# Queries and keys copied out of their banks unscaled, values split at once, and one ordinary step moved in the order of the last part

## The chip, the core and the metric

The kernel runs on one core of one Trainium2 chip. A core has a matrix engine (TensorE, in the profile PE, with PEld for its weight loads), a vector engine (VectorE, DVE), a scalar engine (ScalarE, ACT), GpSimd (POOL) and a queue that issues the transfers (SyncE, SP). The metric is the device time of one execution in microseconds (us); smaller is better.

## What is computed

One encoder block for 256 tokens of width 2048, in float32. The input is normalised and projected once into the heads of three attention mixers and three gates; the mixers are added under their gates, projected, and followed by a SwiGLU feed-forward part of inner width 5632. The reference, cut down:

```python
h = rms_norm(x, g_mix)
qa, ka, va, qb, kb, vb, qc, gt = split(h @ w_in)
qa, ka = rms_norm(split_heads(qa), g_qa), rms_norm(split_heads(ka), g_ka)
oa = mixture of three dilated windows of (qa, ka, va) with rel_bias        # 6 heads
qb, kb = rope(rms_norm(split_heads(qb), g_qb)), rope(rms_norm(split_heads(kb), g_kb))
ob = softmax(qb kb^T / sqrt(128)) vb                                       # 6 query, 2 key heads
kc, vc = split(rms_norm(mem, g_mem) @ w_mem_kv);  kc = rms_norm(kc, g_kc)
oc = softmax(rms_norm(qc, g_qc) kc^T / sqrt(128)) vc                       # 4 heads
merged = sum over branches of sigmoid(gate) * (o @ w_br)
x = x + merged @ w_o
hf = rms_norm(x, g_ffn) @ w_ffn_in
x = x + (silu(hf[:DFF]) * hf[DFF:]) @ w_ffn_out
```

A row's normalisation is a factor per token, so the kernel multiplies with the unscaled x first and applies the factor to the result.

## The kernel before

**Products.** A float32 operand is split into a high and a low part (`split`, lines 128 to 132: ScalarE makes the high part, VectorE the low one), and every product is made of three matmuls: high by high, high by low, low by high. A weight tile of 128 x 1024 comes by DMA into one of six `raw` buffers and is split into `whi` and `wlo`. A plain `product` accumulates two halves of 128 tokens into two banks of 128 x 512. All instructions come from helpers that record the operation, so PE and DMA rows of the trace carry line 75.

**Banks.** There are eight banks of 128 x 512 values, four under the tag "mm" (results of products) and four under "at" (transposes, scores, attention's results). A bank can take its next result when the last reader of the old one is done.

**Stages.** First the memory's keys and values (one `pair`), then eight products for queries, keys and values, each of four heads (`SLOTS`), two gate products with a small branch product each, then, from about 330 us on, the merging of gates and branches, the output projection and the feed-forward part. From there on PE's order is that of the program. Before, while attention runs beside the projections, a scheduler sets each engine's order by its own estimate; `tc.high_priority()` raises what stands under it.

**Heads.** When a product ends, `take_slots` takes its four heads. Queries and keys: ScalarE squares the bank into `sq` (line 576), VectorE sums the squares (577), and once the token factors are known makes `f`; ScalarE reads the bank again, scaled by `f`, into `y` (591); GpSimd applies the gain (612) or VectorE turns the head (604 to 609); PE transposes it (`hT`), and the split gives `headT`. Values are split straight from the bank into `V`, scaled by the token factor (the loop behind `y = rot if turned else y`). The steps between two `yield` run at a tick of the running product; `EVAC_LAG` is three ticks.

**Attention.** `attend` makes scores (`sc`) from two `headT`, the softmax (`pr`), transposes it (`pT`, by `turn`), splits that, and multiplies with `V` into `o`, whose split is `oT`.

**Pairs with seven products.** Behind the early part, `pair` works through a list of steps such as STEPS_LAST. `d` and `D` are ordinary steps (12 matmuls for one weight tile; d into the banks Y and V, D into Z and Q). `f`, `g`, `h`, `p`, `q` make a 2 x 2 block product out of seven products in place of eight: f3, g3 and h3 make the first five for block 3, p0 the sixth and q0 the seventh. f, p and q all use bank X: what p has left there is copied by ScalarE (line 433, `SB`) before q may begin. A step's loads and splits are issued up to four steps ahead of its matmuls. The last part, `feeding` with `last`, has two pairs, both by STEPS_LAST; their results go to x, and out of the core by DMAs in the same queue as the weights.

Of the kernel before, what the change touches and what calls it, by code (L numbers as in the profile page):

```python
# [12 lines left out]
F32R = mybir.dt.float32r  # L13
I32 = mybir.dt.int32
AF = mybir.ActivationFunctionType
ALU = mybir.AluOpType
AX = mybir.AxisListType

P = 128
S = 256  # L20
T = S // P
D = 2048
KT = D // P
HD = 128
# [5 lines left out]
HEAD_LAG, SM_LAG, EVAC_LAG, PV_LAG = 5, 6, 3, 2  # L30
# [24 lines left out]
STEPS_FFN = "d0 D0 d1 D1 d4 D4 f2 d5 g2 D5 h2 f3 d6 g3 h3 p0 D6 q0 d7 D7".split()  # L55
STEPS_O = "d0 D0 d1 D1 f2 d4 g2 D4 h2 d5 f3 D5 g3 d6 h3 p0 D6 q0 d7 D7".split()
STEPS_OUT = "d0 D0 d1 D1 d2 D2 f6 d3 g6 D3 h6 f7 d4 g7 h7 p0 D4 q0 d5 D5".split()
STEPS_LAST = "d0 f2 D0 g2 d1 h2 D1 f3 d4 g3 D4 h3 p0 q0 d5 D5".split()
STEPS_OUT2 = "d0 f5 D0 g5 d1 h5 f6 D1 g6 d2 h6 f7 D2 g7 d3 h7 p0 p2 D3 q0 q2 d4 D4".split()


# [38 lines left out]
def encoder_block(ctx: ExitStack, tc: tile.TileContext, a: dict, out: bass.AP):  # L100
    nc = InOrder(tc)
# [16 lines left out]
    def s4(shape, name, dt=F32):  # L118
        return mid.tile(shape, dt, name=name, tag="s4")

    def bank(name, tag="at"):
        return psum.tile([P, NC], F32, name=name, tag=tag)


    def split(hi, lo, src, scale=None):

        if scale is None:
            nc.scalar.activation(hi, src, AF.Copy)  # L128
            nc.vector.tensor_sub(lo, src, hi.bitcast(F32))  # L129
        else:  # L130
            nc.scalar.activation(hi, src, AF.Copy, scale=scale)
            nc.vector.scalar_tensor_tensor(lo, src, scale, hi.bitcast(F32), op0=ALU.mult, op1=ALU.subtract)  # L132

    def rsqrt(v, shape):

        y = small.tile(shape, F32, name="rs_y")
        h = small.tile(shape, I32, name="rs_h")
        nc.vector.tensor_scalar(h, v.bitcast(I32), 1, None, op0=ALU.logical_shift_right)
        nc.vector.tensor_scalar(y.bitcast(I32), h, -1.0, float(0x5F3759DF), op0=ALU.mult, op1=ALU.add)
        for _ in range(3):  # L140
            t = small.tile(shape, F32, name="rs_t")
            y2 = small.tile(shape, F32, name="rs_y")
            nc.vector.scalar_tensor_tensor(t, y, -0.5, y, op0=ALU.mult, op1=ALU.mult)
            nc.vector.tensor_mul(t, t, v)
            nc.vector.scalar_tensor_tensor(y2, t, 1.5, y, op0=ALU.add, op1=ALU.mult)
            y = y2
        return y
# [104 lines left out]
    known = set()  # L252
# [311 lines left out]
    headT, V = {}, {}  # L564
    s2 = heads.enter_context(tc.tile_pool(name="s2", bufs=16))

    def take_slots(ps, slots, r, name="x"):

        n = sum(s[0][0] != "v" for s in slots)
        if n:  # L570
            y = s4([P, T, 4, HD], "y")
            sq = s4([P, T, 4, HD], "sq")
            ss = small.tile([P, T, 4], F32, name="hss")
            for t in range(T):
                src = ps[t][:, :n * HD].rearrange("p (n d) -> p n d", d=HD)
                nc.scalar.activation(sq[:, t, :n], src, AF.Square)
            nc.vector.tensor_reduce(ss[:, :, :n], sq[:, :, :n], axis=AX.X, op=ALU.add)
            yield EVAC_LAG
        while name not in known:
            yield None  # L580
        if n:
            v = small.tile([P, T, 4], F32, name="hv")
            f = small.tile([P, T, 4], F32, name="hf")
            each = lambda w: r[:, w].unsqueeze(2).broadcast_to([P, T, n])
            nc.vector.tensor_mul(ss[:, :, :n], ss[:, :, :n], each(1))
            nc.vector.tensor_scalar(v[:, :, :n], ss[:, :, :n], 1.0 / HD, EPS, op0=ALU.mult, op1=ALU.add)
            nc.vector.tensor_mul(f[:, :, :n], rsqrt(v[:, :, :n], [P, T, n]), each(0))
            yield EVAC_LAG
            for t in range(T):
                for j in range(n):  # L590
                    nc.scalar.activation(y[:, t, j], ps[t][:, j * HD:(j + 1) * HD], AF.Copy, scale=f[:, t, j:j + 1])
            turned = slots[0][0][1] == "b"
            rot = s4([P, T, 4, HD], "rot") if turned else None
            j = 0
            while j < n:
                m = 1
                while j + m < n and slots[j + m][0] == slots[j][0]:
                    m += 1
                if turned:
                    tab = turns[:, ("qb", "kb").index(slots[j][0])]  # L600
                    for t in range(T):
                        cs, sn = (tab[:, w, t].unsqueeze(1).broadcast_to([P, m, HD]) for w in range(2))
                        yt, other = y[:, t, j:j + m], sq[:, t, j:j + m]
                        nc.vector.tensor_mul(rot[:, t, j:j + m], yt, cs)
                        pairs = lambda v: v.rearrange("p n (d c) -> p n d c", c=2)
                        for c in range(2):
                            nc.vector.tensor_mul(pairs(other)[:, :, :, c], pairs(yt)[:, :, :, 1 - c],
                                                 pairs(sn)[:, :, :, c])
                        nc.vector.tensor_add(rot[:, t, j:j + m], rot[:, t, j:j + m], other)
                else:  # L610
                    g = gh[:, HEAD_GAINS.index(slots[j][0])]
                    nc.gpsimd.tensor_mul(y[:, :, j:j + m], y[:, :, j:j + m],
                                         g.unsqueeze(1).unsqueeze(1).broadcast_to([P, T, m, HD]))
                j += m
            y = rot if turned else y
        for i in range(n, len(slots)):
            v = s2.tile([P, 2, T, HD], F32R, name="V", tag="s2")
            V[slots[i]] = v
            for t in range(T):
                split(v[:, 0, t], v[:, 1, t], ps[t][:, i * HD:(i + 1) * HD], r[:, 0, t:t + 1])  # L620
        if n:
            yield HEAD_LAG
            for j in range(n):
                tp = bank("hT")
                for t in range(T):
                    nc.tensor.transpose(tp[:, t * P:(t + 1) * P], y[:, t, j], ident)
                hT = s2.tile([P, 2, S], F32R, name="headT", tag="s2")
                with tc.high_priority():
                    split(hT[:, 0], hT[:, 1], tp[:, :S])
                headT[slots[j]] = hT  # L630
                if j % 2 and j < n - 1:
                    yield 1
        yield 2
        run_jobs()
# [68 lines left out]
    def run_jobs():  # L703
        while jobs and all(s in headT for s in jobs[0][0] + jobs[0][1]):
            q, k, v, kt = jobs.pop(0)
            start(attend(q, k, v, bias[kt] if kt < 2 else None, kt))
# [5 lines left out]
    def beginning():  # L712
        start(hold(6, row_sums(a["mem"], r_m, 3, "mem")))
        start(hold(10, constants()))
        start(hold(5, fetch(xT, 2)))
        yield pair(block_pair(a["w_mem"], 0), memT, whole_k(KT // 2),
                   lambda c, r: start(take_slots(r, MEM_SLOTS[4 * c:4 * c + 4], r_m, "mem")), operand=memT)
# [4 lines left out]
    for c in range(8):  # L722
        sums = {} if c else {0: row_sums(a["x"], r_x, 4, "x")}
        start(take_slots(product(a["w_qkv"][c], xT, KT, beside=sums), SLOTS[4 * c:4 * c + 4], r_x))
        if c == 0:
            start(biases())
# [41 lines left out]
    def by_pair(these, room):  # L768
        return lambda u, f: (room[these.index(u)][:, 0, (f + 1) % 4], room[these.index(u)][:, 1, (f + 1) % 4])
# [80 lines left out]
    def feeding():  # L850
        for c0, c1 in ((0, 4), (4, 8), (8, KF // 4)):
# [27 lines left out]
            if last:  # L879
                pairs = STEPS_LAST, STEPS_LAST  # L880
                out_forms = by_pair((2, 3), late)
# [114 lines left out]
```

## Time and profile before

| what | value |
|---|---|
| median of 3 runs | 1385.53 us (1384.79 to 1386.54) |
| the profiled execution | 1386.69 us, its span 1384.9 us |
| granted TensorE clock, mean | 0.997 |
| PE busy | 1373.3 us, 99% of the span |
| VectorE, ScalarE busy | 1176.1 us, 829.0 us |
| weights and inputs read | 273.05 MB, 199 GB/s over the span |

How to read it: a timeline row is start, length, engine, line, operation, output<-input, sizes, and in brackets how long the engine sat idle before it and what ended that. Matmuls overlap: a row's length is longer than the distance to the next start. A row of waits is "who waits <- for whom: us in total, times, longest". A row of windows gives the stretch and each engine's busy time in it, then the granted clock, the DMA share and GB/s. A row of groups gives busy us and mean ns behind the first bar, idle us and what ended it behind the second. SPq is the queue of transfers.

### The profile page before, as it was taken

How to read it: one execution, taken by the hardware profiler on the slowest of the kernel's cores; microseconds unless marked ns; L12 is line 12 of the kernel's file. 1: busy time of each engine (PE TensorE's matmuls, PEld its weight loads, DVE VectorE, ACT ScalarE, POOL GpSimd, SP SyncE). 2: the span in 40 equal slices, each digit the busy share in tenths (PEclk: the TensorE clock that was granted, in tenths of full speed). 3: DMA queues.
4: the chain of work that ended last, by engine and by line, in shares of the span. 5: the costliest groups of instructions: out<-in, count | busy, mean ns of one | idle time of the engine just before them, and what ended most of it. 6: DMA issues, size and time to landing. Idle time of an engine off the chain costs nothing.

```text
span 1384.9 us, 17667 instructions
## 1 busy us (share of the span) xinstructions
PE 1373.3 (99%) x6249; PEld 1137.6 (82%) x6249; DVE 1176.1 (85%) x1665; ACT 829.0 (60%) x1131; POOL 14.2 (1%) x14
## 2 busy tenths in 40 slices
PE   9999999999999999999999999999999999999998
PEld 7878878888888888888888888888888888888886
DVE  6869777859988978888988898989998989998997
ACT  7766555655665564656766565655665665566653
POOL 0010001000000000000000000000000000000000
PEclk9999999999999999999999999999999999999999
DMA  9876435556565665755656665665655656565654
GB/s 370 310 244 210 138 126 173 159 162 194 193 231 187 185 229 174 278 170 180 198 183 201 211 192 187 197 213 198 223 186 184 226 179 205 189 202 194 203 169 150
DMA packets 79721, 277.10 MB, mean 200 GB/s; under 512 B 9040, under 2 KB 11600, under 8 KB 79376
## 3 DMA queue, kind: packets, MB, share of 16 engines
q1 hardware_dynamic: 79488, 275.94, 60.6%
q8 instruction: 49, 0.80, 0.2%
q14 instruction: 40, 0.33, 0.1%
q10 hardware_dynamic: 144, 0.02, 0.0%
HBM read 273.05 MB, written 2.88 MB: 199 GB/s over the span
## 4 chain that ended last, share of the span: by engine, by line
PE 97%; DVE 1%; ACT 1%; DMA 0%; issue 0%; SPq 0%; DVEq 0%
PE mmZ L75 17%; PE mmV L75 17%; PE mmY L75 17%; PE mm L75 16%; PE mmQ L75 14%; PE mmX L75 10%; PE mmW L75 3%; PE tp L75 1%; PE sc L75 1%; PE o L75 1%; PE hT L75 0%; DMA raw<-in_w_mem 0%; DVE wlo L129 0%; PE pT L75 0%; ACT whi L128 0%
## 5 line engine op out<-in xcount | busy, mean ns | idle before, releaser
L383 ACT ACTIVATE whi<-raw 128x1024 fp32r<-128x1024 f32 (+1 forms) x480 | 473.6, 998 | 339.1 <-PE mmQ L75 96.7
L393 DVE TENSOR_TENSOR wlo<-raw,whi 128x1024 fp32r<-128x1024 f32 (+1 forms) x480 | 543.0, 1146 | 75.8 <-ACT whi L383 70.5
L75 PE MATMUL mm<-whi,xT 128*128 128x512 f32 x640 | 204.3, 395 | 0.5 <-DVE V L132 0.5
L129 DVE TENSOR_TENSOR wlo<-raw,whi 128x1024 fp32r<-128x1024 f32 x82 | 103.5, 1266 | 52.5 <-ACT whi L128 51.4
L75 PEld LDWEIGHTS mm<-whi,xT 128*128 128x128 f32 x640 | 120.3, 189 | 25.5 <-DVE V L132 1.1
L128 ACT ACTIVATE whi<-raw 128x1024 fp32r<-128x1024 f32 x82 | 86.8, 1065 | 70.1 <-PE mm L75 51.4
L75 PE MATMUL mm<-wlo,xT 128*128 128x512 f32 x320 | 126.4, 395 | 0.0
L393 DVE TENSOR_TENSOR wlo<-t,whi 128x1024 fp32r<-128x1024 f32 x82 | 81.0, 1003 | 40.0 <-ACT whi L383 39.5
L75 PE MATMUL mmY<-whi,x1T 128*128 128x512 f32 x288 | 103.0, 390 | 0.0
L383 ACT ACTIVATE whi<-t 128x1024 fp32r<-128x1024 f32 x82 | 70.5, 877 | 51.2 <-PE mmV L75 31.3
L75 PE MATMUL mmV<-whi,x1T 128*128 128x512 f32 x288 | 100.2, 392 | 0.0
L75 PE MATMUL mmX<-whi,forms 128*128 128x512 f32 x260 | 88.1, 390 | 1.4 <-ACT SB L433 1.4
L75 PE MATMUL mmZ<-whi,x1T 128*128 128x512 f32 x224 | 78.3, 390 | 0.0
L75 PE MATMUL mmQ<-whi,x1T 128*128 128x512 f32 x224 | 78.1, 389 | 0.0
L75 PEld LDWEIGHTS mm<-wlo,xT 128*128 128x128 f32 x320 | 60.7, 190 | 12.5 <-issue 0.7
L75 PEld LDWEIGHTS mmY<-whi,x1T 128*128 128x128 f32 x288 | 54.1, 188 | 11.3
L75 PEld LDWEIGHTS mmV<-whi,x1T 128*128 128x128 f32 x288 | 54.1, 188 | 11.0
L75 PEld LDWEIGHTS mmX<-whi,forms 128*128 128x128 f32 x260 | 48.8, 188 | 12.3 <-ACT SB L433 2.2
L75 PE MATMUL mmV<-wlo,x1T 128*128 128x512 f32 x144 | 56.1, 389 | 0.0
L75 PE MATMUL mmY<-wlo,x1T 128*128 128x512 f32 x144 | 56.0, 389 | 0.0
L75 PE MATMUL mmW<-whi,forms 128*128 128x512 f32 x130 | 51.6, 397 | 0.2 <-DVE x1T L132 0.2
L75 PE MATMUL mmY<-whi,hT 128*128 128x512 f32 x148 | 51.8, 389 | 0.0
(266 smaller groups left out, 2762.4 us busy)
## 6 DMA issues: line engine op xcount, KB each, us to landing
raw<-in_w_ffn SPq DMA_DIRECT2D x176, 512.0 KB, 4.4
raw<-in_w_gate SPq DMA_DIRECT2D x96, 512.0 KB, 4.3
raw<-in_w_ffn_out SPq DMA_DIRECT2D x88, 512.0 KB, 4.4
raw<-in_w_qkv SPq DMA_DIRECT2D x64, 512.0 KB, 4.3
raw<-in_w_o SPq DMA_DIRECT2D x32, 512.0 KB, 4.2
raw<-in_w_br SPq DMA_DIRECT2D x24, 512.0 KB, 4.5
raw<-in_w_mem SPq DMA_DIRECT2D x15, 512.0 KB, 8.0
rawT<-in_memT SPq DMA_DIRECT2D x8, 256.0 KB, 7.6
```

Of the source, the lines that this page charges most:

```text
L75: ins = op(*args, **kw)
L128: nc.scalar.activation(hi, src, AF.Copy)
L129: nc.vector.tensor_sub(lo, src, hi.bitcast(F32))
L383: nc.follow(nc.scalar.activation(hi[:, o], v, AF.Copy))
L393: nc.follow(nc.vector.tensor_sub(*due.pop(0)))
```

## The change

Two things. In `take_slots`, queries and keys are now copied out of their bank as they are, each directly behind its squares (line 578), and scaled from that copy in place (line 601). Squares, copies and their sum are under high priority. The values' split is moved ahead of the scaling, to the place where the token factors are known, and is under high priority too. The lag of three ticks ahead of the factors falls away where these are known already, and one stands now between the values and the rest. In STEPS_LAST, f3 stands one step earlier, and the ordinary step D4 is moved from between g3 and h3 to between p0 and q0.

```diff
-STEPS_LAST = "d0 f2 D0 g2 d1 h2 D1 f3 d4 g3 D4 h3 p0 q0 d5 D5".split()
+STEPS_LAST = "d0 f2 D0 g2 d1 h2 f3 D1 g3 d4 h3 p0 D4 q0 d5 D5".split()
...
-            for t in range(T):
-                src = ps[t][:, :n * HD].rearrange("p (n d) -> p n d", d=HD)
-                nc.scalar.activation(sq[:, t, :n], src, AF.Square)
-            nc.vector.tensor_reduce(ss[:, :, :n], sq[:, :, :n], axis=AX.X, op=ALU.add)
+            with tc.high_priority():
+                for t in range(T):
+                    src = ps[t][:, :n * HD].rearrange("p (n d) -> p n d", d=HD)
+                    nc.scalar.activation(sq[:, t, :n], src, AF.Square)
+                    nc.scalar.activation(y[:, t, :n], src, AF.Copy)
+                nc.vector.tensor_reduce(ss[:, :, :n], sq[:, :, :n], axis=AX.X, op=ALU.add)
+        if name not in known:
             yield EVAC_LAG
         while name not in known:
             yield None
+        with tc.high_priority():
+            for i in range(n, len(slots)):
+                v = s2.tile([P, 2, T, HD], F32R, name="V", tag="s2")
+                V[slots[i]] = v
+                for t in range(T):
+                    split(v[:, 0, t], v[:, 1, t], ps[t][:, i * HD:(i + 1) * HD], r[:, 0, t:t + 1])
         if n:
+            yield EVAC_LAG
...
-                    nc.scalar.activation(y[:, t, j], ps[t][:, j * HD:(j + 1) * HD], AF.Copy, scale=f[:, t, j:j + 1])
+                    nc.scalar.activation(y[:, t, j], y[:, t, j], AF.Copy, scale=f[:, t, j:j + 1])
...
-        for i in range(n, len(slots)):
-            v = s2.tile([P, 2, T, HD], F32R, name="V", tag="s2")
-            V[slots[i]] = v
-            for t in range(T):
-                split(v[:, 0, t], v[:, 1, t], ps[t][:, i * HD:(i + 1) * HD], r[:, 0, t:t + 1])
```

Since a scheduler orders the early part, the order of the engines there changes in many places; from the merging on, up to the last part's two pairs, it stays the same on PE, ScalarE and VectorE. Three places follow.

PE, the head pair of mixer B that shares its product with the first value head; before:

```order
L75 MATMUL mm<-whi,xT 128x512
L75 MATMUL o<-pT,V 128x256
L75 MATMUL pT<-ident,pr 128x128 x4
L75 MATMUL o<-pT,V 128x256 x5
L75 MATMUL pT<-ident,pr 128x128 x4
L75 MATMUL o<-pT,V 128x256
L75 MATMUL mm<-whi,xT 128x512
```

The same heads in the changed program:

```order
L75 MATMUL pT<-ident,pr 128x128 x2
L75 MATMUL o<-pT,V 128x256 x5
L75 MATMUL pT<-ident,pr 128x128 x6
L75 MATMUL mm<-whi,xT 128x512
L75 MATMUL mm<-wlo,xT 128x512
L75 MATMUL mm<-whi,xT 128x512 x2
...
L75 MATMUL mm<-wlo,xT 128x512
L75 MATMUL o<-pT,V 128x256
```

Between the transposes of the softmax (pT) and the product with the values (o) there were no matmuls of the projection; now there are 20.

PE, the last query heads of mixer B; hT is the transpose of the last query, sc its scores; before:

```order
L75 MATMUL pT<-ident,pr 128x128 x4
L75 MATMUL o<-pT,V 128x256 x7
L75 MATMUL hT<-ident,rot 128x128 x2
L75 MATMUL o<-pT,V 128x256 x5
L75 MATMUL sc<-headT 128x256 x2
L75 MATMUL mm<-whi,xT 128x512
```

The same heads in the changed program:

```order
L75 MATMUL pT<-ident,pr 128x128 x8
...
L75 MATMUL mm<-wlo,xT 128x512
L75 MATMUL o<-pT,V 128x256
L75 MATMUL hT<-ident,rot 128x128 x2
L75 MATMUL mm<-whi,xT 128x512 x2
L75 MATMUL mm<-wlo,xT 128x512
L75 MATMUL o<-pT,V 128x256 x11
...
L75 MATMUL mm<-whi,xT 128x512
L75 MATMUL sc<-headT 128x256 x2
```

There are 22 matmuls of the projection between pT and the first o now, and between hT and sc ten of them beside the eleven of o.

PE, the end of the last part's pairs (mmX is the bank of p0 and q0); before:

```order
L75 MATMUL mmX<-wlo,forms 128x512
L75 MATMUL mmX<-whi,forms 128x512 x2
L75 MATMUL mmX<-wlo,forms 128x512
L75 MATMUL mmX<-whi,forms 128x512
L75 MATMUL mmY<-whi,hT 128x512
```

And in the changed program:

```order
L75 MATMUL mmX<-wlo,forms 128x512
L75 MATMUL mmX<-whi,forms 128x512
L75 MATMUL mmZ<-whi,hT 128x512
L75 MATMUL mmZ<-wlo,hT 128x512
...
L75 MATMUL mmQ<-whi,hT 128x512
L75 MATMUL mmX<-whi,forms 128x512
L75 MATMUL mmX<-wlo,forms 128x512
```

The 12 matmuls of D4 (Z and Q) stand between the last one of p0 and the first one of q0, which followed each other before.

In the transfer queue two of the three stores of a bias row (`flat`) had one weight load between them and the loads that fetch the row back; now these follow it directly.

## The prediction

> **What bounds the kernel now.** I read the page first, then the waits of TensorE (PE) and of the load queue, then the timeline wherever two PE starts stand further apart than the work between them.
>
> ```profile
> PE 1373.3 (99%) x6249; PEld 1137.6 (82%) x6249; DVE 1176.1 (85%) x1665; ACT 829.0 (60%) x1131; POOL 14.2 (1%) x14
> 50.57 17.67 PE mm L75 x78
> PE o L75 <- DVE pT L129: 1.7, 2, 0.9
> PE mmX L75 <- ACT SB L433: 1.4, 2, 0.7
> PE sc L75 <- ACT headT L128: 1.0, 1, 1.0
> PE mm L75 <- DVE V L132: 0.5, 2, 0.3
> ```
>
> PE bounds the span, and the change takes no matmul away, so only time that PE loses can be won. The second row (a piece of the chain of waits: 78 matmuls in 17.67 us) gives the undisturbed pace: 0.227 us for 512 columns. For 256 columns I take half, 0.113 us, an estimate. The waits, last number the longest, are short and few. But a wait's figure is idle time against modelled ends, so I measure what each costs by starts: time from start to start less the work between.
>
> **The places where PE loses time, and what the change does to each.**
>
> First place, the second projection of x begins:
>
> ```profile
> 71.94 0.39 PE L75 MATMUL mm<-whi,xT 128*128 128x512 f32 x1
> 72.58 0.50 PE L75 MATMUL mm<-whi,xT 128*128 128x512 f32 x1 [0.26 <-DVE V L132]
> 72.92 0.39 PE L75 MATMUL mm<-wlo,xT 128*128 128x512 f32 x1
> ```
>
> Two starts take 0.98 us where 2 x 0.227 would do: 0.53 us lost. PE waits for a bank that the split of the memory's last value head still reads; the other bank in question was held by the keys until they were scaled. Now the keys leave their bank directly after the squares, nine weight tiles earlier in ScalarE's order, so the product can begin in that bank and asks for the one of the values some matmuls later. I count 0.53 as gone (bounds 0 and 0.53).
>
> Second place, attention:
>
> ```profile
> 153.71 0.60 PE L75 MATMUL pT<-ident,pr 128*128 128x128 f32 x4
> 154.99 0.39 PE L75 MATMUL o<-pT,V 128*128 128x256 f32 x1 [0.68 <-ACT pT L128]
> 155.61 0.50 PE L75 MATMUL mm<-whi,xT 128*128 128x512 f32 x1 [0.23 <-DVE V L132]
> 155.95 0.39 PE L75 MATMUL mm<-wlo,xT 128*128 128x512 f32 x1
> ```
>
> Third place, attention again, with its consequence:
>
> ```profile
> 182.40 0.40 PE L75 MATMUL mm<-whi,xT 128*128 128x512 f32 x1
> 182.64 0.60 PE L75 MATMUL pT<-ident,pr 128*128 128x128 f32 x4
> 182.99 0.36 PE L75 MATMUL o<-pT,V 128*128 128x256 f32 x1
> 184.12 0.98 PE L75 MATMUL o<-pT,V 128*128 128x256 f32 x6 [0.76 <-DVE pT L129]
> 184.94 0.38 PE L75 MATMUL hT<-ident,rot 128*128 128x128 f32 x2
> 185.52 0.68 DVE L129 TENSOR_TENSOR pT<-pT 128x512 fp32r<-128x512 f32 x1
> 186.25 1.18 PE L75 MATMUL o<-pT,V 128*128 128x256 f32 x5 [0.94 <-DVE pT L129]
> 188.44 0.79 PE L75 MATMUL sc<-headT 128*128 128x256 f32 x2 [1.01 <-ACT headT L128]
> 189.03 0.66 PE L75 MATMUL mm<-whi,xT 128*128 128x512 f32 x1
> 193.33 0.44 PE L75 MATMUL mm<-wlo,xT 128*128 128x512 f32 x1
> 170.00:195.00 25.00, 22.30 (x108) 18.45 (x106) 20.07 (x67) 12.71 (x32) 0.00 (x0) 0.86 0.39 125
> ```
>
> Four transposes take 0.35 us (182.64 to 182.99). Second place: 153.71 to 155.95 is 2.24 us for 0.35 + 0.113 + 0.227, so 1.55 us lost. Third place: 182.40 to 193.33 is 10.93 us for one matmul (0.227), four transposes (0.35), twelve of `o` (1.36), two of `hT` (0.175), two of `sc` (0.227) and the ten from 189.03 to 193.33 (2.27): 4.60 us, so 6.33 us lost. Of these 2.03 us are those ten at 0.43 us each; the window's row shows why, a granted clock of 0.86 over 25 us.
>
> Why PE waits here: `o` stands directly behind the transposes whose result it multiplies, and that result must first pass ScalarE and VectorE. From the start of the transposes (182.64) to the end of VectorE's part (185.52 + 0.68) it took 3.56 us, 3.2 us from their end. The order of the changed program (front part) puts 20 matmuls of 512 columns between transposes and `o` at the second place, 4.5 us, and 22 at the third, 5.0 us, both above 3.2. Between the query's last `hT` and `sc` there now stand 10 of 512 columns and 11 of 256: 3.5 us where there were five of 256, 0.6 us. I count both as gone, 1.55 and 6.33 us (bounds 0 and these sums).
>
> Fourth and fifth place, the last part's pairs, where the seventh product (q0) needs the bank from which the sixth (p0) is being copied:
>
> ```profile
> 1340.32 0.39 PE L75 MATMUL mmX<-whi,forms 128*128 128x512 f32 x1
> 1341.39 0.50 PE L75 MATMUL mmX<-whi,forms 128*128 128x512 f32 x1 [0.69 <-ACT SB L433]
> 1341.73 0.40 PE L75 MATMUL mmX<-wlo,forms 128*128 128x512 f32 x1
> 1372.58 0.39 PE L75 MATMUL mmX<-whi,forms 128*128 128x512 f32 x1
> 1373.65 0.50 PE L75 MATMUL mmX<-whi,forms 128*128 128x512 f32 x1 [0.69 <-ACT SB L433]
> 1373.99 0.40 PE L75 MATMUL mmX<-wlo,forms 128*128 128x512 f32 x1
> 1355.93 1.18 SPq L75 DMA_DIRECT2D raw<-in_w_ffn_out  x2
> ```
>
> Each: 1.41 us for two starts, less 0.453: 0.96 us, together 1.91 us. The ordinary step D4 puts 12 matmuls, 2.7 us, over a copy that PE waits for until 1.07 us after the last start; I count all of it. D4's weights are not late: the very last loads of the kernel are issued by 1357.1, 15 us before p0 ends. f3 comes one step earlier, but between it, g3, h3 and p0 there stand as many ordinary steps as before.
>
> **What is added, and what hides it.** Sixteen copies on ScalarE, of the shapes of the squares, and the 56 scalings read SBUF where they read a bank:
>
> ```profile
> L576 ACT ACTIVATE sq<-mm 128x512 f32<-128x512 f32 (+2 forms) x14 | 7.0, 548 | 2.0 <-PE mm L75 1.8
> L591 ACT ACTIVATE y<-mm,hf 128x128 f32<-128x128 f32 x48 | 13.1, 385 | 0.0
> sum 325.00, PE 319.17 PEld 266.12 DVE 237.65 ACT 200.41 POOL 14.19; mean PE 26.60 PEld 22.18 DVE 19.80 ACT 16.70 POOL 1.18
> ACT whi L128 <- PE mm L75: 51.4, 35, 5.9
> ```
>
> 14 squares take 7.0 us, so 16 copies about 8 us. ScalarE is busy 200 of the first 325 us, and its weight splits alone wait 51 us for PE, so 8 us find room: zero on the path. If that cover were gone at a block, one block's two copies, about 1.1 us, would show. A scaling from SBUF has no row; I take the 385 ns from a bank, and even twice that, 21 us more over 325 us, would stay under PE. The value splits keep their number and only come sooner.
>
> **Sum.** 0.53 + 1.55 + 6.33 + 1.91 = 10.3 us. The new order also has some fifteen new places where attention is taken up, and the cheapest wait above cost 0.5 us; I let one such come back: 9.8 us. The profiled execution took 1386.69 us (span 1384.9), 1.16 above the median 1385.53; from that median I forecast 1375.7 us.
>
> **Rivals.** First, the half clock has another cause. Matmuls at half pace came after waits of which none was longer than about 1.0 us, and the two waits of 0.7 us at the end brought none. If it falls anyway, 2.03 us stay: 1377.7 us. [...] The trace speaks rather for several waits close together, since the window at 0.86 is the one that holds the third place.)
>
> Second, a new tight place. The candidates are `sc` 3.5 us behind `hT`, and the last head's `o` with 2.8 us behind its transposes (11 of `o`, 7 of `mm`), below the 3.2 seen. Against it: the 3.2 us came about while ScalarE, which makes all these copies, itself waited for `o`:
>
> ```profile
> ACT oT L128 <- PE o L75: 4.4, 5, 1.3
> ```
>
> It would cost between the second place's 1.55 and the third's 6.33 us: 1377.3 to 1382.0.
>
> Third, the first edit does not do it: these waits come from attention and not from banks, and a small difference in time puts `o` late again. Then only the last part's 1.9 us stay: 1383.6, no measurable difference.
>
> Fourth, slower: the load queue stands still until the bias rows (`flat`) have landed and can be fetched back.
>
> ```profile
> SPq L75 <- DMA flat<-row: 10.8, 3, 4.1
> 123.78 0.38 SPq L75 DMA_DIRECT2D raw<-in_w_qkv  x1
> 127.98 2.54 SPq L75 DMA_DIRECT2D bias<-flat  x4
> SPq L75 <- DVE wlo L129: 119.3, 42, 14.6
> ```
>
> After the second and third `flat` no weight load stands any more before that wait, so one tile goes behind it, 130.5 - 123.8 = 6.7 us later. With no lead at all this costs 2 x 6.7 us and each time a half clock of 2.0: 1375.7 + 17.4 = 1393.1; it decides once the loss passes 9.8 + 2.8 us, 6.3 at each wait. Against it: the queue waits 119 us for tiles to come free, so loads run ahead as far as buffers allow, and ScalarE's splits wait for PE.
>
> **How the numbers follow.** About 0.2%, 2.8 us, is what a measurement here can tell. Forecast 0.63, half clock 0.15, tight place 0.13, only the last part 0.05, load queue 0.04. Faster: the first three but for 0.02 where a tight place and the clock come together, 0.89; same 0.07; slower 0.04. Low: the full 10.3 us from the lowest of three runs, 1384.79, is 1374.5; I put 1374.4. High: 1380.0, through the clock rival and half of the tight place. That holds about 0.8.
>
> **What would show it.** In the changed profile: no PE wait for `pT` or `headT` near 0.7 us or more, PE clock 1.00 in every window behind the start, no wait of mmX for SB, ScalarE's busy time up by some 8 us. I am wrong if the window from 145 to 195 us still shows PE under 24.5 of 25 us, if whi waits for a weight load around 100 to 130 us, or if the same time is lost at other rows of attention.

## The result, and the profile after

The changed kernel takes 1376.7 us in the median of 4 executions (1376.6 to 1377.3), beside 1386.0 us for the kernel before on the same chip (1384.8 to 1386.8): a ratio of 0.9933, 95% interval 0.9921 to 0.9946. That is 9.3 us less; the forecast was 9.8 less, 1375.7 us, with 1374.4 to 1380.0 as its range.

The page of the changed kernel first (span, then busy time by engine), and its waits of TensorE (the whole list):

```profile
span 1375.5 us, 17681 instructions
PE 1368.9 (100%) x6249; PEld 1134.8 (83%) x6249; DVE 1173.3 (85%) x1665; ACT 838.5 (61%) x1147; POOL 13.2 (1%) x14
```

```profile
PE idle L75 <- POOL ident masks.py:199: 1.4, 1, 1.4
PE mmY L75 <- DVE wlo L393: 0.4, 2, 0.2
PE mmY L75 <- ACT whi L383: 0.2, 1, 0.2
PE mmW L75 <- DVE x1T L132: 0.2, 1, 0.2
PE mmZ L75 <- DVE wlo L393: 0.2, 1, 0.2
```

The four waits that the prediction quoted (`o` for `pT`, mmX for `SB`, `sc` for `headT`, mm for `V`) have left the list, and nothing from attention has come in their place. The windows over attention, in which PE had lost most, and the groups of ScalarE from 40 to 330 us:

```profile
145.00:170.00 25.00, 25.00 (x138) 21.49 (x137) 22.08 (x61) 17.53 (x40) 0.00 (x0) 1.00 0.45 147
170.00:195.00 25.00, 25.00 (x131) 21.33 (x129) 19.15 (x48) 13.33 (x25) 0.00 (x0) 1.00 0.50 157
```

```profile
L601 ACT ACTIVATE y<-y,hf 128x128 f32<-128x128 f32 x56 | 17.3, 392 | 1.4 <-DVE hf L597 1.4
L578 ACT ACTIVATE y<-mm 128x512 f32<-128x512 f32 (+2 forms) x14 | 7.6, 543 | 0.4 <-DVE rot L619 0.4
```

PE is busy in all of both windows, with a granted clock of 1.00 where the second had 0.86. The copies take 543 ns each on average. A scaling out of SBUF lasts 392 ns where one out of a bank lasted 385, but these lengths overlap: in a row of scalings the starts lie 293 ns apart here and 250 ns in the kernel before (17.3 us busy for 56, against 15.4 for the same 56). That is some 2 us more in all, the cost for which the prediction had no row.

Between the two profiled executions the span falls by 9.4 us. Part of the gain is hidden by the kernel's beginning, where PE waits for its very first weights (the waits of mmY and mmZ above). The 61st matmul of 512 columns starts at 21.1 us here and at 20.5 us in the kernel before; over the fourteen profiled executions of this study it is 20.0 to 21.1 us, with or without parts of the change. Four of these programs (the heads alone, and three with repeated copies at the very end) have one and the same first part, and in them it lies between 20.4 and 21.0 us. So some 0.6 us of this pair's difference can be the chance of two executions, and 10.0 us were won behind it.

### The profile page after: what moved, and what is told of

The parts are those of the page before. It is cut to its first block, busy times and chain, and to the rows that moved or that the text cites. A ratio compares the mean times of both kernels' runs of the same rounds, so it can differ in the third digit from the quotient of the medians.

```text
span 1375.5 us, 17681 instructions
## 1 busy us (share of the span) xinstructions
PE 1368.9 (100%) x6249; PEld 1134.8 (83%) x6249; DVE 1173.3 (85%) x1665; ACT 838.5 (61%) x1147; POOL 13.2 (1%) x14
## 4 chain that ended last, share of the span: by engine, by line
PE 99%; DMA 0%; DVE 0%; ACT 0%; issue 0%; SPq 0%; DVEq 0%
PE mmZ L75 17%; PE mmV L75 17%; PE mmY L75 17%; PE mm L75 16%; PE mmQ L75 14%; PE mmX L75 10%; PE mmW L75 3%; PE tp L75 1%; PE sc L75 1%; PE o L75 1%; PE pT L75 1%; PE hT L75 0%; DMA raw<-in_w_mem 0%; DVE wlo L393 0%; ACT whi L383 0%; PE bias_ps L75 0%
```

## The experiments

The question is what makes the 9 us. My theory, A: the distance in PE's order between a transposition `pT` and the `o` that uses it; where it is short, PE stands, and where it stands often in a short time, its clock halves. Its rivals: banks that are held too long (B), or small differences that chance has put there. All ratios are against the kernel before on the same chip, with 95% intervals.

### The last part alone

```diff
-STEPS_LAST = "d0 f2 D0 g2 d1 h2 D1 f3 d4 g3 D4 h3 p0 q0 d5 D5".split()
+STEPS_LAST = "d0 f2 D0 g2 d1 h2 f3 D1 g3 d4 h3 p0 D4 q0 d5 D5".split()
```

> Only the order of the last part is changed; the heads and values are taken from their banks as in the kernel before. My theory (the terms are separate): the two waits of mmX for SB go, 2 x 0.96 = 1.9 us, the window from 145 to 195 us keeps its lost 3.6 us and its half clock, the waits of o for pT stay: 1.9 us less than before, ratio 0.9986. A rival, that the time of attention also hangs on small differences anywhere (the order lottery of the prediction), would let the places in attention move or vanish here too, since nothing but chance put them there: up to 9 us less.

Measured: 1383.7 us beside 1386.4, ratio 0.9985 (0.9976 to 0.9993), so 2.7 us less in the median (1.0 to 3.3) where 1.9 were expected. Two rows of its waits of PE and the window of the third place (PE busy, granted clock, DMA share, GB/s):

```profile
PE o L75 <- DVE pT L129: 1.7, 2, 0.9
PE sc L75 <- ACT headT L128: 1.2, 1, 1.2
```

```profile
170.00:195.00 25.00, 22.02 (x109) 0.93 0.36 121
```

No wait of mmX for `SB` is left, and the waits of attention stand where they stood (the clock was halved for one stretch of 3.4 us here and for two in the kernel before, which may be the 0.8 us more than expected; more on that below). What happens in the last part and what happens in attention are two separate gains. PE, ScalarE and VectorE keep the order of the kernel before up to 1323 us in this program, so the run tests chance in the times and not in the order: in that form the rival falls.

### The heads alone

The new `take_slots`, with the old order of the last part.

> The copies, the scaling in place and the early values, with the old order of the last part. My theory: places one to three go (0.53 + 1.55 + 6.33 = 8.4 us), the two waits of mmX for SB stay at 0.7 us each: 8.4 us less than before, ratio 0.9939, and together with the run that changes the last part alone the sum is 10.3 us. Rival, the first edit does not do it by itself: within 2 us of the kernel before, with o again directly behind its pT.

Measured: 1378.9 us, ratio 0.9949 (0.9936 to 0.9961): 7.4 us less, where 8.4 were expected. Of the waits named in the prediction only mmX for `SB` is left (1.4 us, two of 0.7), and every window from 20 to 330 us has a clock of 1.00. With the last part's new order, the full change, it is 2.2 us less again.

### The copies alone, then with the last part

```diff
                 nc.scalar.activation(sq[:, t, :n], src, AF.Square)
+                nc.scalar.activation(y[:, t, :n], src, AF.Copy)
...
-                    nc.scalar.activation(y[:, t, j], ps[t][:, j * HD:(j + 1) * HD], AF.Copy, scale=f[:, t, j:j + 1])
+                    nc.scalar.activation(y[:, t, j], y[:, t, j], AF.Copy, scale=f[:, t, j:j + 1])
```

> Of the change only the copies behind the squares and the scaling in place; no priority for them, and the values are split where they were, last. The smallest distance between a pT and its o in this program's order is 3.85 us of matmuls, above the 3.2 us needed. Theory A (distance in PE's order decides): the second and third place go, 7.9 us less than before, and place one too as far as the keys hold its bank: 8.4 us less, ratio 0.9939. Theory B (it takes the early values and their priority, since the value split is the last reader of a bank): the waits for V stay and less than 2 us is won.

> The copies and the scaling in place with the new order of the last part, values split late and without priority. If the early values and the priority bring nothing of their own: 1378.8 less 2.0 = 1376.8 us, ratio 0.9933 as the changed kernel. If they do: above 1377.5.

Measured: 1378.8 us, ratio 0.9949 (0.9936 to 0.9963), and with the new STEPS_LAST 1377.0 us, 0.9933 (0.9920 to 0.9945). Both are what the versions with early values and high priority take (1378.9 and 1376.7). With the copies in place, the early values and their priority bring nothing that these runs can tell.

### Neither copies nor early values: another lag

```diff
-HEAD_LAG, SM_LAG, EVAC_LAG, PV_LAG = 5, 6, 3, 2
+HEAD_LAG, SM_LAG, EVAC_LAG, PV_LAG = 5, 6, 3, 3
```

> The kernel before with one number changed: o follows its transposes by three steps instead of two. No copy, no early value: banks are held as long as before. Theory A (the distance between pT and its o in PE's order is the cause; it is 3.2 us at the least here): places two and three go with the half clock, 7.9 us less, and only place one's wait for V stays: ratio 0.9943. Theory B (banks held too long are the cause, and the distance is only where it shows): the time lost stays within 2 us of before, at other rows.

Measured: 1379.6 us beside 1386.4, ratio 0.9956 (0.9943 to 0.9968): 6.7 us less by one number. Rows of its timeline at the first two places:

```profile
72.45 0.50 PE L75 MATMUL mm<-whi,xT 128*128 128x512 f32 x1 [0.26 <-DVE V L132]
...
153.09 0.60 PE L75 MATMUL pT<-ident,pr 128*128 128x128 f32 x4
153.64 0.50 PE L75 MATMUL mm<-whi,xT 128*128 128x512 f32 x1
```

```profile
170.00:195.00 25.00, 25.00 (x137) 1.00 0.43 130
```

The wait for the bank of the values is still there, as the edit frees no bank earlier; behind `pT` there now stands an `mm` and no `o`, and the clock is full. Theory B predicted under 2 us of gain here and falls: in this kernel's order the banks are not what costs the 6 to 8 us, the distance is.

> Two edits of one line each on the kernel before: o three steps behind its transposes instead of two, and the new order of the last part. No copy, no early value. If the terms add (6.75 us by the first alone, about 2 by the second alone): 1377.6 us beside 1386.4 before, ratio 0.9937 to 0.9941, and what is left to the changed kernel (0.9933) is the 0.53 us of place one. Rival, the copies bring something of their own that the lag does not: over 1379, ratio above 0.995.

The edits are that number and the new STEPS_LAST. Measured: 1377.5 us, ratio 0.9940 (0.9926 to 0.9954). Two one-line edits have all but 0.5 us of what the copies with the new last part reach (1377.0), a difference within the spread of the two (1377.1 to 1378.3, and 1376.8 to 1377.8), and the profile of this run still has the first place, 0.53 us by starts, and one other wait for a bank (0.2 us, for a scaling of `y`). So the copies have one thing of their own, the early bank at the first place, and for the rest are one way among others to another order of PE.

### Early values without the copies

The change with two lines taken back: no copy, and the scaling reads the bank; the old STEPS_LAST.

```diff
-                    nc.scalar.activation(y[:, t, :n], src, AF.Copy)
...
-                    nc.scalar.activation(y[:, t, j], y[:, t, j], AF.Copy, scale=f[:, t, j:j + 1])
+                    nc.scalar.activation(y[:, t, j], ps[t][:, j * HD:(j + 1) * HD], AF.Copy, scale=f[:, t, j:j + 1])
```

> The changed kernel's early values and their priority without the copies (queries and keys are scaled out of their bank as before), with the old order of the last part; to be set against the run that has the copies too (heads_only, 0.9949). Theory A (distances in PE's order decide): in this order two of the o stand 1.0 and 0.7 us behind their transposes, near 146 us, and the third product of the first block asks for its bank 0.45 us after the last reader; waits of some 2.5 us near 150 and of up to 2.7 near 90 us, perhaps with 2.0 us of half clock: 1383 to 1386 us, ratio 0.9975 to 0.9995. Rival B (the early values alone free the banks, copies are not needed): as heads_only, 0.995.

Measured: 1386.4 us, ratio 1.0005 (0.9996 to 1.0014). All of the heads' 7.4 us is gone, a little more than theory A gave it. PE, then ScalarE, at the third product:

```profile
96.50 0.73 PE L75 MATMUL bias_ps<-ones,reps 64*128 64x512 f32 x2
100.64 0.79 PE L75 MATMUL mm<-whi,xT 128*128 128x512 f32 x1 [3.42 <-ACT y L600]
101.23 0.63 PE L75 MATMUL mm<-wlo,xT 128*128 128x512 f32 x1
101.66 0.63 PE L75 MATMUL mm<-whi,xT 128*128 128x512 f32 x1
```

```profile
95.20 2.94 ACT L128 ACTIVATE whi<-raw 128x1024 fp32r<-128x1024 f32 x3
98.04 0.57 ACT L358 ACTIVATE row<-bias_ps 128x511 f32<-128x511 f32 x1
98.52 1.06 ACT L577 ACTIVATE sq<-mm 128x512 f32<-128x512 f32 x2
99.47 2.13 ACT L600 ACTIVATE y<-mm,hf 128x128 f32<-128x128 f32 x8
```

```profile
95.00:120.00 25.00, 21.58 (x86) 0.86 0.66 202
```

Here a bank does decide: the eight scalings that empty two banks, four for each, stand behind weight splits on ScalarE. PE waits 3.4 us, until the first four are done (100.6), and then makes thirteen matmuls at half clock, 2.7 us more. The first place's wait (0.5 us) and one `o` shortly behind its `pT` at 161 us (1.3 us by starts) make up the rest. So the early values need the copies: alone they move the loss to another row. Rival B of this run falls, and so does any short rule, "banks" or "distance" alone: each new order has to be looked through for both.

### How near may o stand?

The changed kernel with one lag changed: HEAD_LAG 2 in place of 5, or PV_LAG 1 in place of 2.

> The changed kernel with one number changed: heads are turned two steps behind their scaling instead of five. Banks are freed as early as in the changed kernel. In this order one o stands directly behind its transposes (0.0 us), one 2.5 us behind. Theory A (distance decides): waits of 3.2 and 0.7 us near 172 us, so 1380.6 us, and 1382.6 if the clock halves behind them; ratio 0.9960 to 0.9975. Rival B (banks decide): as the changed kernel, 0.9933.

> The changed kernel with o one step behind its transposes instead of two. In this order one o alone stands near, 1.1 us behind its transposes (at about 197 us), all others 4.5 us or more. Theory A: one wait of 2.1 us, 1378.8 us, ratio 0.9948; bank theory: as the changed kernel, 0.9933. For the half clock: if it comes from waits that stand close together, this single one brings none (the window's clock stays 1.00); if one long wait is enough, 2.0 us more, 1380.8.

Measured: 1381.3 us, ratio 0.9966 (0.9953 to 0.9978), and 1377.2 us, ratio 0.9937 (0.9924 to 0.9950). The direction is theory A's: banks are as early as in the changed kernel, and yet the first of the two loses 4.6 us. The size is not. PE and VectorE where `o` stands 0.0 us behind its transposes (the first run), then PE, ScalarE and VectorE where it stands 1.1 us behind (the second):

```profile
179.22 0.60 PE L75 MATMUL pT<-ident,pr 128*128 128x128 f32 x4
181.56 0.36 PE L75 MATMUL o<-pT,V 128*128 128x256 f32 x1 [1.74 <-DVE hv L596]
182.40 0.87 PE L75 MATMUL o<-pT,V 128*128 128x256 f32 x5 [0.48 <-DVE pT L129]
```

```profile
179.87 1.22 DVE L129 TENSOR_TENSOR wlo<-raw,whi 128x1024 fp32r<-128x1024 f32 x1
181.40 0.34 DVE L132 SCALAR_TENSOR_TENSOR V<-mm,scales,V 128x128 fp32r<-128x128 f32 x1
181.66 0.68 DVE L129 TENSOR_TENSOR pT<-pT 128x512 fp32r<-128x512 f32 x1
```

```profile
203.11 0.60 PE L75 MATMUL pT<-ident,pr 128*128 128x128 f32 x4
204.71 1.28 PE L75 MATMUL o<-pT,V 128*128 128x256 f32 x6
```

```profile
203.75 0.60 ACT L128 ACTIVATE pT<-pT 128x512 fp32r<-128x512 f32 x1 [0.53 <-PE pT L75]
```

```profile
204.38 0.69 DVE L129 TENSOR_TENSOR pT<-pT 128x512 fp32r<-128x512 f32 x1
```

In the second run neither engine has anything long in front of its part, and `pT` is whole at 204.38 + 0.69 = 205.07, 1.6 us after the transposes' end (203.11 + 0.35, as the prediction counts it). In the first, `wlo` (1.22 us), the low part of an `oT` (0.41) and a value split stand in front of VectorE's part: `pT` is whole at 182.34, 2.8 us after the end. (The 1.74 us ahead of the first `o` is put down to `hv`, another result in that queue; the `o` behind it waits for `pT` itself.) The 3.2 us from which the prediction argued came about in the same way in the kernel before, on both engines:

```profile
182.89 1.06 ACT L128 ACTIVATE whi<-raw 128x1024 fp32r<-128x1024 f32 x1 [0.62 <-ACT pT L128]
183.85 0.58 ACT L128 ACTIVATE pT<-pT 128x512 fp32r<-128x512 f32 x1
184.38 1.22 DVE L129 TENSOR_TENSOR wlo<-raw,whi 128x1024 fp32r<-128x1024 f32 x1
```

ScalarE was in a weight split when the transposes ended (182.99) and began its part 0.86 us later, where the second run took 0.29 us. That part was done at 184.43; VectorE had just begun a weight split and came to `pT` at 185.52. The distance needed was thus no constant: 1.6 us at the place where both engines were free, 2.8 and 3.2 us at the two where one or both stood behind a weight split. For that reason the second run loses 0.3 us (0.42 us between its first two `o`, which otherwise lie 0.12 apart) where I expected 2.1.

The executions of the first run also differ among each other: 1379.6 us where it was profiled (each window's clock 1.00), and 1380.9 to 1381.5 in the five others, four of them with a mean clock of 0.998 against the profiled one's 0.999. The five have no profile, but their times and mean clock fit the half clock, in some executions and not in others.

### When does the clock halve?

The run with the heads alone keeps two lone stops of PE at the end, where mmX waits for `SB`. There the copy is repeated, which lengthens each stop and changes nothing else in PE's order:

```diff
-                            copy(("B", 0), "X")
+                            for _ in range(3 if order is STEPS_LAST else 1):
+                                copy(("B", 0), "X")
```

> The run with the copies and the old order of the last part (heads_only, 1378.9 us), in whose last part TensorE stops twice, 32 us apart, for 0.96 us until SB is copied. Here that copy is made three times over into the same place, so each stop grows by 2 x 0.49 us to 1.94 us; nothing else changes in TensorE's order. Theory A (a stop of about 2 us can bring the half clock by itself, since after_hd2 lost 2.0 and 0.7 us and halved in most executions): between 1380.9 and 1384.9 us, executions 2.0 us apart by the number of halvings. Theory B (the clock halves only when TensorE does almost nothing for about 3.4 us, as it did in no_copies): 1380.9 us, clock 1.00 in all executions.

> The same with five copies: stops of 0.96 + 4 x 0.49 = 2.92 us, each by itself. Theory A: both halve the clock in most executions, 1378.9 + 3.9 + 2 x 2.0 = 1386.8 us. Theory B (only about 3.4 us of rest do): 1382.9 us, clock 1.00.

> The same with seven copies: stops of 0.96 + 6 x 0.49 = 3.90 us. Both theories: the clock halves behind both stops, 1378.9 + 5.9 + 4.0 = 1388.8 us; if a window with a fixed beat decides, not in all executions.

Measured: 1383.2 us (executions 1381.8 to 1386.9), 1387.9 us (1386.0 to 1390.2) and 1390.6 us (1390.5 to 1391.9). Both stops of the first of them, PE's rows, then ScalarE's copies:

```profile
1332.50 0.39 PE L75 MATMUL mmX<-whi,forms 128*128 128x512 f32 x1
1335.64 0.50 PE L75 MATMUL mmX<-whi,forms 128*128 128x512 f32 x1 [2.75 <-ACT SB L433]
1336.20 0.63 PE L75 MATMUL mmX<-whi,forms 128*128 128x512 f32 x2
1337.28 0.63 PE L75 MATMUL mmY<-whi,hT 128*128 128x512 f32 x1
1337.70 0.63 PE L75 MATMUL mmY<-wlo,hT 128*128 128x512 f32 x1
...
1368.43 0.39 PE L75 MATMUL mmX<-whi,forms 128*128 128x512 f32 x1
1370.77 0.57 PE L75 MATMUL mmX<-whi,forms 128*128 128x512 f32 x1 [1.95 <-ACT SB L433]
1371.13 0.63 PE L75 MATMUL mmX<-wlo,forms 128*128 128x512 f32 x1
```

```profile
1334.37 1.22 ACT L433 ACTIVATE SB<-mmX 128x512 f32<-128x512 f32 x2
...
1368.86 1.86 ACT L433 ACTIVATE SB<-mmX 128x512 f32<-128x512 f32 x3 [0.98 <-PE mmX L75]
```

The stops are longer than I had reckoned: a repeated copy took 0.62 us (1.86 for three) and not 0.49, and at the first stop a weight split slipped in between. By starts, less one matmul, PE loses here 2.9 and 2.1 us; with five copies 4.2 and 3.4; with seven 5.4 and 4.6. All six brought the half clock in the profiled executions (0.427 us from start to start; above at the second stop at once, at the first only 1.3 us after PE had started again). Without it these three would take 1378.9 plus what the stops grew by: 1382.3, 1384.8 and 1387.3 us.

- Three copies: from about that time (the lowest four of eleven executions, 1381.8 to 1382.6) to 4.6 us above it.
- Five copies: all are 1.2 to 5.4 us above.
- Seven copies: all are 3.3 to 4.6 us above, about twice 1.7 us, what 3.4 us at half clock cost if they are filled with matmuls (an estimate, half of them).

A stop of 2 to 3.5 us halved the clock in some executions, one of 4.2 us or more in all that were measured, as far as their times tell, and one of 0.85 us in none (two such stops in each of the fifteen executions of the runs with the heads alone, the copies alone and the lag alone, all with a mean clock of 1.000). Theory B of the first two runs, that it takes about 3.4 us of rest, falls; so does A as I had put it, by the length of a stop.

What stood ahead of each half clock is seen when the trace is cut at the places where the clock changes. Here is the kernel before, then the run with three copies (the stretch, PE busy, granted clock, DMA share, GB/s):

```profile
183.17:186.58 3.41, 1.71 (x12) 1.00 0.43 147
186.58:190.00 3.42, 2.41 (x10) 0.50 0.51 156
190.00:193.41 3.41, 3.41 (x10) 0.50 0.00 0
193.41:196.82 3.41, 3.41 (x18) 1.00 0.00 0
```

```profile
1333.52:1336.93 3.41, 1.29 (x6) 1.00 0.02 6
1336.93:1340.34 3.41, 3.41 (x10) 0.50 0.00 0
...
1367.65:1371.06 3.41, 1.46 (x7) 1.00 0.00 0
1371.06:1374.47 3.41, 3.41 (x9) 0.50 0.00 0
```

In these and the other traces every stretch at half clock between the kernel's start and its end is 3.413 us long, or twice that, and the distance between two of them in one trace is a whole multiple of 3.413 us (30.72 us in the run with three copies, nine times). I cut all fourteen traces of this study into windows of that length, one behind the other from a change of the clock on, and took each matmul as its undisturbed pace (0.227 us for 512 columns and 0.11 for a transposition by the starts of rows; half of 0.227 for 256 columns, and twice all this at half clock, are estimates, beside 0.12 and 0.427 us from start to start). The first window of each trace and the one in which its matmuls end are left out. PE's share of work in a window, against the clock of the next:

```
windows at full clock: 5586
  next at half clock (9):   0.00 0.15 0.19 0.26 0.33 0.34 0.34 0.36 0.38
  next at full clock, lowest of 5577:   0.42 0.53 0.56 0.65
windows at half clock: 14
  next at half clock (5):   0.03 0.59 0.60 0.63 0.66
  next at full clock (9):   0.95 and more
```

In both states the two groups stand apart. The fourteen windows in which the matmuls end agree: the clock was half behind 0.02 to 0.37 (seven of them) and full behind 0.41 to 0.84 (seven). So in these traces a full clock was followed by the half one behind every window with 0.38 of work or less and behind none with 0.41 or more. A half clock was followed by the full one behind windows with 0.95 or more; behind 0.59 to 0.66 it stayed, though behind 0.53 and 0.56 a full clock had stayed full. The rows above at 183.17 and 1333.52 have 0.33 and 0.34, that at 186.58 has 0.60. What follows for stops is an estimate from these numbers: with 0.38 of work a window of 3.413 us has lost 2.1 us, with 0.41 it has lost 2.0. A stop of 0.85 us is less than that; one of 2.1 to 3.4 can take as much if it falls into one window; one of 4.2 or more leaves 2.1 us in one of two wherever the cut lies. And three waits of 0.9 to 1.3 us by starts, as in the third place, can or can't, by where the cut falls among them. In the first run of the last section, in the execution that was profiled, the cut fell through the two waits, and the window kept 0.42.

## Why the prediction was right

- **First place, 0.53 us.** Right by the traces. It is there in every run without the copies (the row at 72.45 us above) and in none with them. The times can't tell so little: the pair of runs that differ by it most closely, the lag or the copies with the new last part, stands 0.5 us apart (1377.5 and 1377.0), within their spread, and the former has a second wait for a bank as well.
- **Second and third place, 1.55 and 6.33 us.** Right in cause, somewhat too large. The copies alone, or the lag alone, which leaves the banks as they were, each remove them. By the lag it was 6.7 us of the 7.9; by the heads or the copies, with the first place, 7.4 to 7.6 of the 8.4. Of the differences 0.5 us is the half clock, counted whole (next point). Another 0.3 us is a misread row: the prediction takes 0.35 us for four transposes (182.64 to 182.99), but a row of four lasts 0.60 us and a single one 0.27, so their starts lie 0.11 us apart and the four take 0.44; the `o` at 182.99 starts under the last of them. With that, 0.22 for two `hT` and 0.12 us from one `o` or `sc` to the next, the two places lose 1.46 and 6.10 us. In the lag's run 0.2 us stay behind the transposes at 153.09; the rest, at most 0.2 us, is within what two medians differ by.
- **The half clock, 2.03 us within the third place.** Right in size, wrong as a certainty. Of 51 executions of the kernel before that stood beside these experiments, 12 had a mean granted clock of 1.000 and took 1384.1 to 1385.4 us, median 1384.5; the other 39 had 0.997 to 0.999 and took 1385.7 to 1387.7, median 1386.5. The groups don't overlap, and their medians lie 2.0 us apart. Most of this kernel's spread is thus the half clock coming or not, and it comes three times in four; the sum should have had 0.76 x 2.03 = 1.5 us. By their times (1384.8, 1385.5 and 1386.5) the three executions behind the forecast's 1385.53 mixed both kinds, and its sum was made from one that had it.
- **Fourth and fifth place, 1.91 us.** Right: 2.1 us (1379.6 to 1377.5), 1.8 (1378.8 to 1377.0) and 2.2 (1378.9 to 1376.7) in three pairs of runs without the half clock. The fourth pair, the last part alone against the kernel before, has 2.7 us, with the half clock's chance in both.
- **What is added.** Right in its result: ScalarE's busy time rose by 9.5 us for the 8 forecast, all of it hidden. The copies were busy for 8.8 us. The scalings out of SBUF were not free, as the prediction's 385 ns each would have them, but some 2 us more than out of a bank, well under the 21 us of its bound.
- **The 0.5 us allowed for a new wait in attention.** Not needed. No such wait came. But the sum of 10.3 us was some 0.8 us too large, 0.5 by the half clock and 0.3 by the transposes, so that an allowance for something else brought the forecast's 9.8 us near the measured 9.3 is luck. The forecast time is 1.0 us too low: 0.5 us lies in the gain, and 0.5 in its base, 1385.5 where the median with one execution more is 1386.0.
- **Rival, half clock by another cause.** Fell: with the waits gone the clock is 1.00 in all windows, and in the run with three copies each of the two longer stops brought the half clock (0.50 for 3.41 us behind each). I had given this rival 0.15, an estimate, since none of the waits here was longer than about 1.0 us; but five of the nine full-clock windows that stood ahead of a half clock had 0.33 to 0.38 of work, so a rest of 3.4 us was not needed. My own reason, waits close together, was right for this place; what told the two groups of windows apart in all traces is the share of work in 3.413 us. By the mean clocks, the same program halved in some executions and not in others (39 and 12 of the 51).
- **Rival, a new tight place.** Did not come, though the step that guarded against it was mis-sized: "3.2 us needed" was what stood in the queues of ScalarE and VectorE at that one place, and 1.6 to 3.2 is the measured span. Nor was ScalarE waiting for `o` there, as the prediction says; it was in a weight split (the row at 182.89). The forecast held since 4.5 and 5.0 us lie above all of that span; that the last head's 2.8 us, inside it, was enough is in part luck.
- **Rivals, the first edit does nothing, and the load queue.** Both fell. With the first edit alone (the heads alone) 7.4 us are won. The queue waits for `flat` about as long as before in all (11.1 us for 10.8, the longest 5.2 for 4.1), and no wait of PE for a weight of the projections followed:

```profile
SPq L75 <- DMA flat<-row: 11.1, 3, 5.2
```

What stays open: why the copies make the scheduler set another order in attention. The lag run shows that their work as such isn't needed for it, and no run takes apart what the scheduler weighed.

## What to carry to other kernels

When the bound engine is at 99%, add up its lost time by start-to-start distances, place by place, and ask of each place whether a program order or a buffer causes it; a change that seems to free buffers may win mostly by reordering, and then one lag can be as good as sixteen copies. Count the consequence too: here a stretch of 3.4 us in which PE worked 0.38 of the time or less was paid a second time, by the half clock behind it (2.03 us at the third place), and the executions of the kernel before fell into two groups with their mean clock (1.000, and 0.997 to 0.999). When an edit is made of parts, try the parts alone: here early values without the copies gave back all that the copies win.

## What the chip showed that was not expected

- The clock in the fourteen traces of this study: its stretches at half speed lasted 3.413 us or twice that and lay whole multiples of it apart. It was half behind each full-clock window with 0.38 of work or less and behind none with 0.41 or more, and full again behind 0.95 and more (behind 0.66 it was not). The ten matmuls at half clock in the third place took 2.03 us more than at their pace. One program, with three copies at the end, took 1381.8 to 1386.9 us in eleven executions; that the cuts between windows fall differently in each would explain it, but only one of them has a profile.
- Two squares on ScalarE into different places took 1.06 us together (the run with early values alone), their starts 0.48 us apart in the kernel before; two copies into the same place took 1.22 us and three 1.86 (the run with three copies), 0.62 us apart, without that overlap of some 0.1 us. Whether the common place causes it was not taken apart.
- The next scaling of 128 x 128 started 293 ns behind one that read SBUF (the changed kernel) and 250 ns behind one that read a bank (the kernel before), though the two lasted 392 and 385 ns. The 56 of them kept ScalarE busy for 17.3 and 15.4 us, by the distance of their starts, where their lengths add up to 22.0 and 21.7.
